# The eight steps of a second modulation, moved between the stages of four token blocks

## The chip, the cores and the metric

The kernel runs on one core of a Trainium2 chip. The metric is the device time of one execution in microseconds (us). "Before" is the kernel as it stood, "after" the one with the change.

## The reference

One layer of a streaming encoder for 2048 prompt tokens and 64 sample tokens, width 1024, all in float32. A vector `c` for each of the two sequences gives six modulation vectors of 1024 values; everything else is per token:

```
mod = silu(c) @ w_ada + b_ada                  # 1024 -> 6 x 1024
sh1, sc1, gt1, sh2, sc2, gt2 = split(mod, 6)
h = rms_norm(x) * (1 + sc1) + sh1
glu_a, glu_b, q, k, v, g_conv, g_attn = split(h @ w_in)
conv = silu(layer_norm(depthwise31(glu_a * sigmoid(glu_b)))) @ w_conv_out
attn = band_attention(norm(q), norm(k), v) @ w_attn_out
x = x + gt1 * ((sigmoid(g_conv) * conv + sigmoid(g_attn) * attn) @ w_o)
h2 = rms_norm(x) * (1 + sc2) + sh2
x = x + gt2 * ((silu(gate) * up) @ w_ffn_out)  # gate, up = split(h2 @ w_ffn_in)
```

`sh1` and `sc1` are needed at once. `gt1`, `sh2`, `sc2` and `gt2`, here called the second modulation, are needed only when all of `q` to `g_attn` has been computed for every token.

## The kernel before

**Stages.** The first half of the program runs over four blocks of tokens (576, then three of 512). A block passes eight stages, given by `ORDER` (line 564): the products q, k and v; four gated products, numbered 0 to 3 (`glu`: two products of 24 matmuls on 512 tokens each, then a tanh gate, after which VectorE adds up the 31 taps of the convolution); and "g", the sixteen gates. They stand in the order q, 0, k, 1, v, 2, 3, g. The second half (merge, output product, feed-forward) comes after all four blocks. A float32 product is made of three matmuls on split operands: a high part `hh`/`whi` in float32r and a low part `hl`/`wlo`.

**Order.** TensorE's instructions stand in the order in which the Python code emits them. While the code emits a product, it keeps an estimate of each engine's load, and at fixed distances it lets other work in (`Stream`, `Lane`): the attention heads of the block before (`sc` scores, `ptp` transposed probabilities, `po` outputs), the norm of the next block (`pt<-ident,x_t`), and the rows of q and k, whose normed form `kn` is transposed back (`pt<-ident,kn`) and stored. So an instruction added or removed on TensorE shifts the places of the rest. The other engines run their own queues in order. Nearly all DMAs are issued from one queue, SyncE's (SP).

**The second modulation.** `mod_steps` is a generator with eight steps, one for each half of the four vectors. A step multiplies four slabs of `w_ada` (`wmod`, 512 KB each, 256 rows by 512 columns) by the two `c` vectors: 16 instructions on TensorE, 32 matmul records in the trace. VectorE copies the sums (`R<-pa`), two small products with `sel` follow some 2.5 us later by the estimate, and VectorE writes one of `B2`, `A2`, `gates_c`. The slabs live in four buffers: `Slabs.free` fills a buffer as soon as the step that used it is done, so the 2 MB for a step are requested right behind the step before it, from SP's queue. The first step's slabs are there long before.

**Where the steps stand.** `MODS` (line 562) says after which stages a step is emitted; the loop over `ORDER` ends with

```
        for _ in range(MODS.get((b, stage), 0)):
            next(mods)
    next(mods)
```

The last `next(mods)` stands behind all stages: it transposes and stores the gates.

**Two buffers for split rows.** `parts()` hands out pairs `part_h`, `part_l` from two buffers (`NS = 2`). ScalarE writes the high part, VectorE the low part, and a pair is free again when its DMA to DRAM has landed. The convolution's last step (`c_d<-part_h`, four of them at the end of a block), the rows of q and k (`q_d`, `k_d`) and the finished heads (`o_d`) all go through these two.

Of the kernel before, what the change touches and what calls it, by code (L numbers as in the profile page):

```python
# [558 lines left out]


MOD_HALVES = [(c6, half) for c6 in (3, 4, 2, 5) for half in range(2)]
MODS = {(b, ct): 1 for b in (1, 2) for ct in range(4)}

ORDER = [(b, st) for b in range(4) for st in ("q", 0, "k", 1, "v", 2, 3, "g")]

# [57 lines left out]
def streaming_layer(ctx: ExitStack, tc: tile.TileContext, I, O):  # L623
# [1024 lines left out]
    for b, stage in ORDER:  # L1648
# [44 lines left out]
        else:  # L1693
# [7 lines left out]
            if stage == 3:  # L1701
# [3 lines left out]
                else:  # L1705
                    tail.add(conv_norm(y, 0, QB, lo))
        for _ in range(MODS.get((b, stage), 0)):
            next(mods)
# [673 lines left out]
```

## Time and profile before

| | before |
|---|---|
| median of 3 runs | 2945.97 us |
| lowest and highest run | 2940.69 and 2946.77 us |
| profiled execution, its own time | 2941.67 us |
| its span, first to last instruction | 2939.5 us |
| TensorE, VectorE, ScalarE, GpSimd busy | 98%, 70%, 46%, 40% of the span |
| TensorE busy between 300 and 960 us | 650.53 of 660 us |
| granted TensorE clock, mean | 0.997 |

Times in the profile count from the start of the span. In a timeline, a row has the start and the duration in us, the engine, the line, the operation, what it writes and reads, and in brackets the idle time of the engine just before it with what ended that. Line 105 is that of a helper that records every instruction, so rows are told apart by the names of their tiles. PE is TensorE, PEld its weight loads, DVE VectorE, ACT ScalarE, POOL GpSimd, SPq SyncE's DMA queue.

### The profile page before, as it was taken

How to read it: one execution, taken by the hardware profiler on the slowest of the kernel's cores; microseconds unless marked ns; L12 is line 12 of the kernel's file. 1: busy time of each engine (PE TensorE's matmuls, PEld its weight loads, DVE VectorE, ACT ScalarE, POOL GpSimd, SP SyncE). 2: the span in 40 equal slices, each digit the busy share in tenths (PEclk: the TensorE clock that was granted, in tenths of full speed). 3: DMA queues.
4: the chain of work that ended last, by engine and by line, in shares of the span. 5: the costliest groups of instructions: out<-in, count | busy, mean ns of one | idle time of the engine just before them, and what ended most of it. 6: DMA issues, size and time to landing. Idle time of an engine off the chain costs nothing.

```text
span 2939.5 us, 44832 instructions
## 1 busy us (share of the span) xinstructions
PE 2889.3 (98%) x16193; PEld 2587.5 (88%) x16193; DVE 2053.9 (70%) x3648; ACT 1362.7 (46%) x2453; POOL 1164.9 (40%) x753
## 2 busy tenths in 40 slices
PE   7999999999999999999999999999999999999999
PEld 5899777888888887988999998999999999999998
DVE  5897788668967885577777756666666557566666
ACT  3346543751564266563444345444444345444442
POOL 1201210111011002553566452366567742465667
PEclk9999999999999999999999999999999999999999
DMA  9989899978996987984444875332333965333333
GB/s 322 315 305 314 287 281 329 285 232 306 285 297 197 320 270 224 291 295 157 144 144 146 292 261 200 97 122 94 115 115 104 346 220 179 97 103 106 115 107 127
DMA packets 467067, 628.04 MB, mean 214 GB/s; under 512 B 36196, under 2 KB 314584, under 8 KB 466845
## 3 DMA queue, kind: packets, MB, share of 16 engines
q1 hardware_dynamic: 452944, 606.11, 63.4%
q10 hardware_dynamic: 13901, 19.08, 1.9%
q8 instruction: 127, 2.08, 0.3%
q14 instruction: 95, 0.78, 0.1%
HBM read 476.53 MB, written 148.54 MB: 213 GB/s over the span
## 4 chain that ended last, share of the span: by engine, by line
PE 47%; DVE 2%; ACT 1%; DMA 1%; issue 1%; POOL 0%; SPq 0%; ACTq 0%; DVEq 0%; POOLq 0%
PE ps L105 29%; PE pd L105 13%; PE pw L105 5%; DVE wlo L105 1%; ACT whi L105 1%; DVE ps L105 0%; DMA cin<-o_d 0%; DMA x<-x_d 0%; DVE acc L105 0%; ACT xn L105 0%; DMA wst<-in_w_ffn_in 0%; DMA wfo<-in_w_ffn_out 0%; DMA tg<-g_d 0%; DVE sums L105 0%; PE pt L105 0%
## 5 line engine op out<-in xcount | busy, mean ns | idle before, releaser
L105 PE MATMUL ps<-t,whi 128*128 128x384 f32 (+1 forms) x2112 | 502.0, 322 | 2.8 <-ACT u L105 1.7
L105 POOL TENSOR_TENSOR wlo<-wst,whi 128x1024 fp32r<-128x1024 f32 (+1 forms) x159 | 362.7, 2293 | 246.1 <-ACT whi L105 214.4
L105 ACT ACTIVATE whi<-wst 128x1024 fp32r<-128x1024 f32 (+1 forms) x265 | 258.3, 979 | 316.1 <-PE ps L105 129.6
L105 PE MATMUL ps<-b,whi 128*128 128x384 f32 (+1 forms) x1584 | 380.7, 325 | 6.4 <-DVE v L105 2.1
L105 PEld LDWEIGHTS ps<-t,whi 128*128 128x128 f32 x2112 | 367.8, 188 | 10.1 <-ACT u L105 3.9
L105 DVE SCALAR_TENSOR_TENSOR y<-u,wd,y 128x512 f32<-128x512 f32 (+1 forms) x480 | 370.1, 774 | 8.0
L105 PE MATMUL ps<-hh,whi 128*128 128x512 f32 (+2 forms) x992 | 362.8, 366 | 0.1
L105 DVE TENSOR_TENSOR acc<-acc,pd 128x512 f32<-128x512 f32 x482 | 322.2, 685 | 48.1 <-PE pd L105 45.6
L105 PE MATMUL ps<-hh,wlo 128*128 128x512 f32 (+2 forms) x992 | 345.2, 348 | 0.0
L105 PE MATMUL ps<-hl,whi 128*128 128x512 f32 (+2 forms) x992 | 344.5, 347 | 0.0
L105 PE MATMUL ps<-t,wlo 128*128 128x384 f32 (+1 forms) x1056 | 338.5, 321 | 0.0
L105 PE MATMUL pd<-whi,hid 128*128 128x512 f32 x912 | 297.9, 391 | 0.6 <-DVE hid L105 0.3
L105 PEld LDWEIGHTS ps<-b,whi 128*128 128x128 f32 x1584 | 276.9, 188 | 14.6 <-DVE v L105 3.2
L105 ACT ACTIVATE pr<-pr,sm 128x640 f32<-128x640 f32 (+3 forms) x272 | 201.9, 749 | 137.1 <-DVE sm L105 134.8
L105 PE MATMUL ps<-b,wlo 128*128 128x384 f32 (+1 forms) x792 | 256.1, 323 | 0.0
L105 POOL TENSOR_TENSOR r<-t,mhalf 128x1 f32<-128x1 f32 (+2 forms) x68 | 82.3, 1219 | 403.7 <-DVE t L105 377.8
L105 PEld LDWEIGHTS ps<-hh,wlo 128*128 128x128 f32 x992 | 186.5, 188 | 22.6
L105 DVE TENSOR_TENSOR wlo<-wst,whi 128x1024 fp32r<-128x1024 f32 (+1 forms) x106 | 135.9, 1286 | 100.3 <-ACT whi L105 98.9
L105 PEld LDWEIGHTS pd<-whi,hid 128*128 128x128 f32 x912 | 171.2, 188 | 37.2 <-DVE acc L105 1.8
L105 PEld LDWEIGHTS ps<-hh,whi 128*128 128x128 f32 x992 | 187.0, 189 | 18.2 <-issue 3.3
L105 PEld LDWEIGHTS ps<-hl,whi 128*128 128x128 f32 x992 | 187.4, 189 | 14.3 <-issue 1.7
L105 PEld LDWEIGHTS ps<-t,wlo 128*128 128x128 f32 x1056 | 198.2, 188 | 0.8
(233 smaller groups left out, 6309.6 us busy)
## 6 DMA issues: line engine op xcount, KB each, us to landing
whi<-w_din_h SPq DMA_DIRECT2D x72, 512.0 KB, 6.4
wlo<-w_din_l SPq DMA_DIRECT2D x72, 512.0 KB, 7.3
wst<-sum_d SPq DMA_DIRECT2D x131, 256.0 KB, 3.1
wfo<-in_w_ffn_out SPq DMA_DIRECT2D x64, 512.0 KB, 4.1
wmod<-in_w_ada SPq DMA_DIRECT2D x46, 512.0 KB, 8.8
sum_d<-ws SPq DMA_DIRECT2D x88, 256.0 KB, 2.0
wst<-in_w_ffn_in SPq DMA_DIRECT2D x85, 256.0 KB, 3.2
wst<-in_w_in SPq DMA_DIRECT2D x40, 512.0 KB, 6.0
```

The source lines that it names most:

```text
L105: self.last = f(*args, **kw)
```

## The change

```
-MODS = {(b, ct): 1 for b in (1, 2) for ct in range(4)}
+MODS = {at: 1 for at in ((0, "g"), (1, 0), (1, 1), (1, 2), (1, "g"), (2, 0), (2, 1), (2, 2))}
```

Before, the steps stand behind the gated products 0, 1, 2, 3 of block 1 (steps 1 to 4) and of block 2 (steps 5 to 8). Now step 1 stands behind the gates of block 0, steps 2 to 4 behind products 0 to 2 of block 1, step 5 behind the gates of block 1, and steps 6 to 8 behind products 0 to 2 of block 2. Behind the products numbered 3 stands none. What a step computes is unchanged, and so is the number of instructions on TensorE.

On TensorE, at the passage from the gates of block 0 (`128x288`, one half of its 576 tokens) to q of block 1 (`128x512`), a piece of the difference reads:

```order
 L105 MATMUL ps<-hl,whi 128x288
 L105 MATMUL ps<-hh,wlo 128x288
-L105 MATMUL ps<-whi,hh 128x512
-L105 MATMUL ps<-wlo,hh 128x512
-L105 MATMUL ps<-whi,hl 128x512
-L105 MATMUL ps<-whi,hh 128x512
-L105 MATMUL ps<-wlo,hh 128x512
-L105 MATMUL ps<-whi,hl 128x512
+L105 MATMUL pa<-wmod,cl 32x256 x16
```

Step 1 now comes before the first matmul of q in block 1; the removed rows are found again behind it.

SP's queue around products 2 and 3 of block 1, before. `whi` and `wlo` are the two parts of a stored weight slab, `wmod` the slabs of a step, `o_d` a finished head:

```order
L479 DMA whi<-w_din_0_h 128x1024
L479 DMA wlo<-w_din_0_l 128x1024
L249 DMA wmod<-in_w_ada 128x2x512 x4
L1460 DMA o_d<-part_h 128x64
L1460 DMA o_d<-part_l 128x64
L479 DMA whi<-w_din_1_h 128x1024
L479 DMA wlo<-w_din_1_l 128x1024
L479 DMA whi<-w_din_0_h 128x1024
L479 DMA wlo<-w_din_0_l 128x1024
L249 DMA wmod<-in_w_ada 128x2x512 x4
```

The same place after:

```order
L1460 DMA o_d<-part_h 128x64
L1460 DMA o_d<-part_l 128x64
L479 DMA whi<-w_din_0_h 128x1024
L479 DMA wlo<-w_din_0_l 128x1024
L249 DMA wmod<-in_w_ada 128x2x512 x4
L479 DMA whi<-w_din_1_h 128x1024
L479 DMA wlo<-w_din_1_l 128x1024
L479 DMA whi<-w_din_0_h 128x1024
L479 DMA wlo<-w_din_0_l 128x1024
```

Before, two groups of four slabs are requested here: for step 4, which stands right behind the next product, and for step 5. Now there is one, for step 5, and its user stands behind the gates of the block.

VectorE's queue at product 0 of block 1, before. `u` is the gated product, `y` a tap of the convolution, `part_l<-ln` the low part of the third and fourth stores to `c_d`, `part_l<-pt` a row of q, `kn` the next row of q that TensorE will transpose:

```order
L105 SCALAR_TENSOR_TENSOR u<-tb,ps 128x512
L105 RECIPROCAL sm<-sm 128x1
L105 TENSOR_SCALAR y<-u,wd,cols 128x512
L105 RECIPROCAL sm<-sm 128x1
L105 COPY R<-pa 128x256
L105 TENSOR_TENSOR part_l<-ln,part_h 128x512 x2
L105 SCALAR_TENSOR_TENSOR part_l<-pt,gqk,part_h 128x512
L105 TENSOR_TENSOR kn<-kn,r 128x512
```

The same place after:

```order
L105 SCALAR_TENSOR_TENSOR u<-tb,ps 128x512
L105 TENSOR_SCALAR y<-u,wd,cols 128x512
L105 SCALAR_TENSOR_TENSOR y<-u,wd,y 128x512
L105 TENSOR_TENSOR part_l<-ln,part_h 128x512
L105 COPY R<-pa 128x256
L105 SCALAR_TENSOR_TENSOR y<-u,wd,y 128x512
L105 TENSOR_TENSOR part_l<-ln,part_h 128x512
L105 SCALAR_TENSOR_TENSOR y<-u,wd,y 128x512
L105 SCALAR_TENSOR_TENSOR part_l<-pt,gqk,part_h 128x512
L105 TENSOR_TENSOR kn<-kn,r 128x512
```

Three taps (`y<-u,wd,y`) now stand ahead of `kn` that stood behind it; two small reciprocals are gone from there; and `R`, which waits for the step's sums, stands behind the first `part_l` instead of ahead of both.

## The prediction

> **What bounds the kernel now.** I read the head of the page first, then the waits of TensorE between 300 and 800 us, where all eight steps stand before and after, then the timelines at the waits. The head of the page gives the span and the busy time of each engine:
>
> ```profile
> span 2939.5 us, 44832 instructions
> PE 2889.3 (98%) x16193; PEld 2587.5 (88%) x16193; DVE 2053.9 (70%) x3648; ACT 1362.7 (46%) x2453; POOL 1164.9 (40%) x753
> ```
>
> TensorE (PE) is busy for 98% of the span, and its work is the same before and after. So the change can only move what TensorE waits for and what the clock gate takes. Its waits between 300 and 800 us, as the total, the count and the longest:
>
> ```profile
> PE pt L105 <- DVE kn L105: 4.0, 1, 4.0
> PE pa L105 <- DMA wmod<-in_w_ada: 2.6, 4, 0.7
> PE sc L105 <- DVE sm L105: 1.6, 2, 1.3
> PE ps L105 <- DVE hl L105: 0.6, 1, 0.6
> ...
> PE pt L105 <- DVE x_t L105: 0.2, 1, 0.2
> ```
>
> Two of them belong to steps. The slabs `wmod` are waited for four times, 2.6 us in all, and the timeline shows that all four stand at one step, number 4, behind product 3 of block 1:
>
> ```profile
> 466.28 0.39 PE L105 MATMUL ps<-hh,wlo 128*128 128x512 f32 x1
> 467.23 0.64 PE L105 MATMUL pa<-wmod,cl 128*32 128x256 f32 x8 [0.56 <-DMA wmod<-in_w_ada]
> 468.49 0.64 PE L105 MATMUL pa<-wmod,cl 128*32 128x256 f32 x8 [0.62 <-DMA wmod<-in_w_ada]
> 469.82 0.64 PE L105 MATMUL pa<-wmod,cl 128*32 128x256 f32 x8 [0.69 <-DMA wmod<-in_w_ada]
> 471.19 1.08 PE L105 MATMUL pa<-wmod,cl 128*32 128x256 f32 x8 [0.73 <-DMA wmod<-in_w_ada]
> 472.20 0.80 PE L105 MATMUL ps<-hh,whi 128*128 128x512 f32 x1
> ```
>
> Products and slabs come from one queue (SP). It requests a step's four slabs right behind the step before. These are the requests for steps 3 and 4:
>
> ```profile
> 416.62 2.43 SPq L249 DMA_DIRECT2D wmod<-in_w_ada  x4
> 457.12 3.14 SPq L249 DMA_DIRECT2D wmod<-in_w_ada  x4
> ```
>
> Step 4's request stands at 457.12 to 460.26 and its first matmul is due at 466.51 (the last product matmul at 466.28 and one spacing of 0.23): 9.4 us from the first slab and 6.3 us from the last. What a slab takes there, from the DMA view between 440 and 480 us (KB each, and the median time to landing):
>
> ```profile
> q1 hardware_dynamic: 6546, 14.49, 102.3%
> wmod<-in_w_ada SPq DMA_DIRECT2D x8, 512.0 KB, 10.1
> ```
>
> A slab lands after 10.1 us in a queue that is full, and the step asks after 9.4. The other steps are not waited for.
>
> **The change, part by part.** *Step 4 moves from behind product 3 to behind product 2.* Before, the step took until 472.20. Without a wait a step takes as long as step 1 behind product 0, the first two of these rows, which also show the wait for `kn`:
>
> ```profile
> 353.73 1.94 PE L105 MATMUL pa<-wmod,cl 128*32 128x256 f32 x32
> 355.59 0.50 PE L105 MATMUL ps<-whi,hh 128*128 128x512 f32 x1
> ...
> 356.16 0.39 PE L105 MATMUL ps<-whi,hl 128*128 128x512 f32 x1
> 360.51 0.63 PE L105 MATMUL pt<-ident,kn 128*128 128x128 f32 x4 [3.96 <-DVE kn L105]
> ```
>
> 355.59 - 353.73 = 1.86 us. So step 4 should have ended at 466.51 + 1.86 = 468.37 and ended at 472.20, 3.83 us late. The windows from 466.51 on add the clock (busy times with counts, then PEclk, the share of the DMA engines and GB/s):
>
> ```profile
> 356.39:360.51 4.12, 0.16 (x1) 0.03 (x1) 2.51 (x4) 1.46 (x3) 0.00 (x0) 1.00 0.77 206
> 361.56:368.39 6.83, 6.83 (x24) 5.86 (x23) 4.71 (x11) 3.13 (x6) 0.00 (x0) 0.50 1.08 387
> 466.51:470.80 4.29, 2.07 (x25) 0.50 (x24) 3.17 (x7) 1.75 (x3) 0.67 (x1) 1.00 1.06 397
> 470.80:474.21 3.41, 3.02 (x14) 1.92 (x15) 0.42 (x1) 0.00 (x0) 0.00 (x0) 0.50 1.03 413
> 480.00:490.00 10.00, 10.00 (x52) 8.33 (x51) 10.00 (x19) 5.44 (x10) 0.45 (x1) 1.00 0.78 202
> ```
>
> From 470.80 to 474.21 the clock was 0.50. The part behind 472.20, 2.01 us, did half the work: another 1.0. This whole stall, 4.8 us, is at stake. Afterwards step 4 stands where step 3 stood, and step 3 where step 2 stood. The slabs of step 4 are then requested about as step 3's were, at 416.62, for a use at about 452.54:
>
> ```profile
> 452.54 1.29 PE L105 MATMUL pa<-wmod,cl 128*32 128x256 f32 x20
> ```
>
> That is 36 us against 10.1. What hides them is a whole product and the stage v; if that cover went, they would cost up to the 3.8 again. Every other step has as long: step 5 stands behind the gates, a product later than step 4, whose 144 matmuls of 0.23 us alone are 33 us, and steps 6 to 8 repeat 2 to 4. I take **-4.8**; the bounds are 0 and -4.8.
>
> The Trainium skill (TensorE: Matmul & The Clock Gate, "HAM oscillation — how this bites in real kernels") says that the clock falls when TensorE idles for more than about 3.4 us on end; by it this term is -3.8, since the longest gap here is 0.73 us. The trace disagrees: 0.50 was granted after a stretch in which TensorE was busy for 2.07 of 4.29 us in short pieces. At `kn`, where the gap is 3.96 us, rule and trace agree.
>
> *Step 1 moves to the gates of block 0.* It adds 1.86 us ahead of q of block 1. The slabs have been there from the start. The norm's waits `hl` 0.6 and `x_t` 0.2 stand near this passage, and 1.86 us of TensorE's work ahead of them gives their engines time: **-0.8**, bounds 0 and -0.8.
>
> *Step 2 stands where step 1 stood, and the wait for `kn` behind it is looked at again.* TensorE came at 356.39 (356.16 and a spacing) and waited until 360.51 for VectorE. What VectorE and ScalarE did there:
>
> ```profile
> 354.32 0.68 DVE L105 SCALAR_TENSOR_TENSOR u<-tb,ps 128x512 f32<-128x512 f32 x1
> 356.17 0.69 DVE L105 TENSOR_TENSOR part_l<-ln,part_h 128x512 fp32r<-128x512 f32 x1
> 357.19 0.69 DVE L105 TENSOR_TENSOR part_l<-ln,part_h 128x512 fp32r<-128x512 f32 x1 [0.33 <-ACT part_h L105]
> 359.02 0.75 DVE L105 SCALAR_TENSOR_TENSOR part_l<-pt,gqk,part_h 128x512 fp32r<-128x512 f32 x1 [1.13 <-ACT part_h L105]
> 359.68 0.68 DVE L105 TENSOR_TENSOR kn<-kn,r 128x512 f32<-128x512 f32 x1
> 358.26 0.69 ACT L105 ACTIVATE part_h<-pt,gqk 128x512 fp32r<-128x512 f32 x1 [1.10 <-DMA c_d<-part_h]
> 362.54 0.69 ACT L105 ACTIVATE part_h<-pt,gqk 128x512 fp32r<-128x512 f32 x1 [3.59 <-DMA c_d<-part_h]
> ```
>
> `kn` stands behind a `part_l` that needs a `part_h`, which waits for one of the two buffers, that is for a store to `c_d` to land. The stores were issued at these times:
>
> ```profile
> 356.16 0.32 SPq L1350 DMA_DIRECT2D c_d<-part_h  x1
> ...
> 357.80 0.41 SPq L1350 DMA_DIRECT2D c_d<-part_h  x1
> ```
>
> The first freed its buffer after 2.1 us (358.26 - 356.16), the second after 4.7 (362.54 - 357.80). After the change three more taps stand ahead of `kn`, at the mean of their group (busy total, mean ns, idle ahead):
>
> ```profile
> L105 DVE SCALAR_TENSOR_TENSOR y<-u,wd,y 128x512 f32<-128x512 f32 (+1 forms) x480 | 370.1, 774 | 8.0
> ```
>
> 3 x 0.77 = 2.3 us more. They fill VectorE's idle 0.33 + 1.13 = 1.5 us; `u`, which started 0.59 us behind the product's end at 353.73, no longer has a score and a reciprocal ahead of it in a row, for 0.5 or so. That leaves about **+0.3**: TensorE still waits, for 4.3 us, and the clock still falls (0.50 over 6.83 us, at most 3.4 lost). The bounds are far apart. If the queue has caught up before `u`, the 4.1 of wait and 3.4 of clock go, -7.5. If the stores land late, it costs more: pairs of parts from 300 to 400 us took
>
> ```profile
> DMA to landing us min/median/max: 4.6/7.1/8.1
> ```
>
> from issue to landing. That is the slower rival below. I stay at +0.3, because the rows at this very place give it.
>
> *The catch-up behind product 3.* While TensorE stalled at step 4, VectorE got 3.83 us in which it fell no further behind. In 480 to 490 it is busy for 10.00 of 10.00 us. Without the stall the scores and heads of the next stage could find it late: between 0 and +3.8. The nearest row for what such a wait costs is `sc <- sm`, 1.6 us over two; the two waits stand over 500 us of similarly full stretches, so I take **+0.3**.
>
> The sum: -4.8 - 0.8 + 0.3 + 0.3 = -5.0. The profiled execution took 2941.67 us by its own time (2939.5 of span and 2.2 around it), 4.3 below the median of the three runs, 2945.97, which spread from 2940.69 to 2946.77. I take the sum from the middle of the two, 2943.8: **2938.8 us**.
>
> The Trainium skill (DMA: Bandwidth & Descriptors, "Anatomy of one DMA — SWDGE (gpsimd) path") puts a transfer at 2.0 us and its bytes at 436 GB/s, 3.2 us for a slab of 512 KB. By it the last slab of step 4, requested by 460.26, would have landed by 463.5, ahead of 466.51, and the term would be nil. The queue is another one, and the trace disagrees: 10.1 us, and four waits.
>
> **The rivals.** *B: the wait for `kn` goes too.* For it: the third and fourth stores may go out earlier. Against it: three more taps. Price at best -7.5 - 0.3 more than the forecast, 2931.0; half of it, with the wait below what makes the clock fall, 2935.
>
> *C: the step's stall is given back.* VectorE's lack of reserve in 480 to 490 turns most of the 4.8 into waits for `sm` and `pl` behind product 3. For it: 10.00 of 10.00. Against it: of 200 us with such stretches only 1.9 us of waits came from it. The net is -1 to 0, about 2943.
>
> *D: slower, by the two buffers.* In the new order a request for a 512 KB slab of the products stands among the halves of the stores to `c_d`. If the two stores then land after 7.1 to 8.1 us instead of 2.1 and 4.7, the chain to `kn` is later by (8.1 - 2.1) + (8.1 - 4.7) = 9.4 us. Then the stall falls into two, one for each store, and a second stretch at clock 0.50 like that of 6.83 us loses 3.4 more: +12.8 at this place. With the 5.3 saved elsewhere (4.8 + 0.8 - 0.3 for the catch-up) the net is +7.5, 2951.3; half as much again at step 6 in block 2, whose place is alike, makes 2957. Slower than the median by over 0.2% it is from 13.1 above the forecast, which needs a little of the second place. For it: the queue is at 0.77 to 1.08 in these very rows. Against it: the second late store delayed nothing of TensorE's before, since `kn` for it had passed.
>
> *E: the change does not do what it says.* The wait for slabs goes from step 4 to another step: 2943.
>
> **How the numbers follow.** About 0.2%, 5.9 us, is what a measurement of this kernel can tell from no change (its runs differ by 6.1). The bounds are 2940.1 and 2951.9 against the median. The forecast, 0.50, lies 1.3 us below the lower one: 0.33 faster, 0.17 same. B 0.15 is faster. C 0.09 and E 0.02 are same. D 0.24 is slower: with the second place it clears the bound by far, and without it it reaches 2951.3, where a queue a little later decides. Together 0.48 faster, 0.28 same, 0.24 slower. The range goes from B's best, 2931.0, to D at its first place alone, 2951.5; D's upper part, 0.17, and little of the rest lie outside.
>
> **What would show it.** Right: TensorE's waits between 300 and 800 us hold no `wmod`; the clock stays at 1.00 behind product 3 of block 1; the wait for `kn` behind product 0 is still there at 4 to 4.5 us; `hl` and `x_t` are gone. Wrong, faster: no wait for `kn` (B). Wrong, slower: a wait for `kn` of over 8 us, or one in block 2, released by `part_h` after a store to `c_d` (D); or new waits for `sm` and `pl` at 470 to 500 (C).

## The result: slower, and the profile after

| | before | after |
|---|---|---|
| median of 6 runs each, beside one another | 2944.61 us | 2954.56 us |
| lowest and highest | 2940.69 and 2946.77 | 2950.42 and 2955.94 |
| ratio, 95% interval | | 1.0036 (1.0024 to 1.0047) |
| profiled execution, its span | 2939.5 | 2948.5 |

The changed kernel is about 10 us slower. The head of its page shows that no engine has more to do:

```profile
span 2948.5 us, 44833 instructions
PE 2889.5 (98%) x16193; PEld 2586.4 (88%) x16193; DVE 2053.3 (70%) x3648; ACT 1363.8 (46%) x2453; POOL 1165.5 (40%) x753
```

TensorE is busy for 2889.5 us, as before for 2889.3. Nearly all of the 9 us between the two spans are waits. TensorE's waits between 300 and 800 us after the change:

```profile
PE sc L105 <- DMA kk<-k_d: 5.9, 1, 5.9
PE sc L105 <- DVE sm L105: 4.8, 3, 3.2
PE pt L105 <- DVE kn L105: 3.6, 1, 3.6
PE sc L105 <- issue: 0.9, 1, 0.9
...
PE ps L105 <- DMA wlo<-w_dqkv_l: 0.2, 1, 0.2
```

The waits for `wmod`, `hl` and `x_t` that stood here are gone, as meant. In their place stand a wait of 5.9 us for `kk`, the load of a head's keys, and one of 3.2 us for `sm`, a score bank that VectorE has not freed yet. The timeline gives the places: `sm` in q of block 1, the known wait for `kn` behind product 0, and `kk` in the gates of block 1:

```profile
345.27 0.51 PE L105 MATMUL sc<-kk,q 128*128 128x256 f32 x2 [3.17 <-DVE sm L105]
368.92 0.63 PE L105 MATMUL pt<-ident,kn 128*128 128x128 f32 x4 [3.65 <-DVE kn L105]
492.05 1.41 PE L105 MATMUL sc<-kk,q 128*128 128x320 f32 x4 [5.87 <-DMA kk<-k_d]
```

The clock fell behind each of the three, as the windows show (the last three columns are PEclk, DMA share, GB/s):

```profile
345.80:349.21 3.41, 3.41 (x10) 2.75 (x10) 0.94 (x5) 1.44 (x4) 0.00 (x0) 0.50 0.97 326
369.69:373.10 3.41, 3.41 (x12) 2.75 (x11) 1.61 (x3) 1.67 (x3) 0.00 (x0) 0.50 1.08 306
489.15:495.98 6.83, 3.93 (x12) 3.37 (x13) 1.58 (x5) 0.69 (x1) 1.41 (x2) 0.50 0.84 254
```

Half of the busy time in them was lost: 1.7, 1.7 and 2.0 us. The loss behind `kn` was there before, with 3.4 us; the other two are new.

To compare kernels closer than their total times allow, I use the passage in which they differ. TensorE's matmul records have the same order in all of them up to number 1950 of 16193 (in the gates of block 0) and in the last 10698 (from the gates of block 2 on). The table has the time from the start of record 1950 to that of the first of the last 10698, and in it TensorE's idle time and half of its busy time in stretches at clock 0.50, worked out from the traces.

| profile | passage us | idle | lost to the clock |
|---|---|---|---|
| before, first and second | 654.5, 653.4 | 9.1, 9.4 | 4.9, 3.4 |
| after, first and second | 662.8, 668.0 | 16.8, 18.7 | 5.4, 8.9 |

In the first profiles 8.3 of the 9.0 us lie in this passage: 7.7 of idle time and 0.5 of clock. The second pair (n1_before and n2_after, below) has the same long waits at the same places (after the change `sm` 3.5, `kn` 3.6 and `kk` 5.9 us), so they belong to the order and not to one execution; what varies is mostly the clock.

### The profile page after: what moved, and what is told of

Its sections match the earlier page's. It is cut to its first block, busy times and chain, and to the rows that moved or that the text cites. A ratio compares the mean times of both kernels' runs of the same rounds, so it can differ in the third digit from the quotient of the medians.

```text
span 2948.5 us, 44833 instructions
## 1 busy us (share of the span) xinstructions
PE 2889.5 (98%) x16193; PEld 2586.4 (88%) x16193; DVE 2053.3 (70%) x3648; ACT 1363.8 (46%) x2453; POOL 1165.5 (40%) x753
## 4 chain that ended last, share of the span: by engine, by line
PE 47%; DVE 2%; DMA 1%; ACT 1%; issue 1%; POOL 0%; SPq 0%; ACTq 0%; DVEq 0%
PE ps L105 29%; PE pd L105 13%; PE pw L105 5%; DVE wlo L105 1%; ACT whi L105 0%; DVE ps L105 0%; DMA x<-x_d 0%; DMA cin<-o_d 0%; DMA wst<-in_w_conv_out 0%; ACT xn L105 0%; DVE acc L105 0%; DMA wfo<-in_w_ffn_out 0%; DMA tg<-g_d 0%; DVE sums L105 0%; PE pt L105 0%
## 5 line engine op out<-in xcount | busy, mean ns | idle before, releaser
L105 POOL TENSOR_TENSOR r<-t,mhalf 128x8 f32<-128x8 f32 (+2 forms) x68 | 83.8, 1240 | 404.0 <-DVE t L105 379.8
```

What stands on the lines that cost most here:

```text
L105: self.last = f(*args, **kw)
```

## The experiments

**Parts of the change.** Each moves only some of the steps; all else is as before. Step 1 and the steps of block 2 get the places that the change gives them. Step 4 does not: the change puts it behind product 2, which step 3 leaves, while here it goes behind the gates. What the two have in common is that no step stands behind product 3 of block 1. No part moves steps 2 and 3.

```
step 4:   MODS at (1,0) (1,1) (1,2) (1,"g")      (2,0) (2,1) (2,2) (2,3)
step 1:   MODS at (0,"g") (1,1) (1,2) (1,3)      (2,0) (2,1) (2,2) (2,3)
block 2:  MODS at (1,0) (1,1) (1,2) (1,3) (1,"g") (2,0) (2,1) (2,2)
step 5:   MODS at (1,0) (1,1) (1,2) (1,3) (1,"g") (2,1) (2,2) (2,3)
```

Step 4 alone: 

> Only step 4 moves, from behind product 3 of block 1 to behind its gates; steps 1 to 3 and 5 to 8 stand as before, so TensorE's order is that of before up to 466 us. Theory (each move has its own price, and this is the one that gains): the four waits for wmod and the clock loss behind them go, 3.8 + 1.0 = -4.8 us against before, about 2939.8; no wait for kk in the gates, since no slabs of a step are requested there ahead of the loads of q and kk. Rival (any shift of the order of the attention heads behind product 3 makes a new wait): the wmod waits go but waits for sm or kk of 3 to 8 us appear between 470 and 540 us, 2943 to 2948.

Step 1 alone: 

> Only step 1 moves, from behind product 0 of block 1 to behind the gates of block 0; steps 2 to 8 stand as before. Theory (the move of step 1 makes the wait for sm in q of block 1): a wait of sc for sm of about 3.2 us near 345 us with half clock behind it (1.7 us), step 4's waits for wmod still there; 3 to 5 us above before, 2947.5 to 2949.5. Rival (the wait for sm in the changed kernel comes from the place of step 2, behind product 0, or from chance): no wait above 1 us for sm near 345, and 0.8 us below before, 2943.8.

The steps of block 2: 

> Only the steps of block 2 move: step 5 to behind the gates of block 1, steps 6 to 8 to behind products 0 to 2 of block 2; steps 1 to 4 stand as before, with the waits for wmod at step 4. Theory: nothing in block 2 waits before or after; the small waits that the changed kernel has behind 600 us (0.9, 1.3 and 0.6) come with this part, so 0 to 2.4 us above before, 2944.6 to 2947. Rival (the wait for kk in the gates of block 1 belongs to step 5's new place): a wait for kk of 4 to 6 us near 490, 2951 or more.

Of these, step 5 alone: 

> Only step 5 moves, from behind product 0 of block 2 to behind the gates of block 1; steps 1 to 4 and 6 to 8 stand as before. With all four steps of block 2 moved the time was 5 us above before. Theory (step 5 is the one that costs, by 1.86 us ahead of the norm and q of block 2, as step 1 does in block 1): 3 to 5 us above before, with waits for x_t, hl or sm between 590 and 680 us. Rival (steps 6 to 8, each a product earlier, cost it): no change, within 1.5 us of before.

| moved | ratio to before (95%) | passage | idle | clock |
|---|---|---|---|---|
| step 4 | 0.9992 (0.9983 to 1.0001) | 652.9 | 10.0 | 1.7 |
| step 4, repeated | 0.9990 (0.9981 to 0.9999) | 655.7 | 10.2 | 5.8 |
| step 1 | 1.0024 (1.0012 to 1.0035) | 660.9 | 14.8 | 4.4 |
| steps of block 2 | 1.0017 (1.0008 to 1.0026) | 655.8 | 11.0 | 3.4 |
| step 5 | 1.0006 (0.9997 to 1.0015) | 659.2 | 12.3 | 6.4 |

With 2944 us as 1, step 4 is worth -2.4 and, repeated (

> Step 4 alone moved, once more. If its gain is real, 2 to 4 us below before again; if the first comparison was chance, within 1.5 us of before.

), -2.9 us; step 1 costs +7.1; the steps of block 2 cost +5.0. With the mean of the first two that is +9.5 together, against +10.6 by the ratio for the whole change. That does not show the change to be the sum of its parts. Besides the place of step 4, its longest wait, 5.9 us for `kk`, stands in none of them: near 490 us only step 1's part has one, of 1.3 us. What is shown is the sign of each: an empty place behind product 3 gains a little, and the two other moves lose.

Step 1 brings the wait for `sm` and a longer one for `kn`, as the first four rows of its waits between 300 and 800 us show:

```profile
PE sc L105 <- DVE sm L105: 6.3, 6, 3.4
PE pt L105 <- DVE kn L105: 5.5, 1, 5.5
PE pa L105 <- DMA wmod<-in_w_ada: 1.4, 2, 0.7
PE sc L105 <- DMA kk<-k_d: 1.3, 1, 1.3
```

The 5.5 is the 4.0 of before and the 1.86 us of the step that no longer stands ahead of it, less 0.4. In the change itself step 2 stands there, and the wait for `kn` is 3.6; so not all of the 7.1, which is above the expected 3 to 5, belongs to the change. In step 4's rows, here the first three of the repeat, there is no `wmod`, but 3.2 us for `kk` have come:

```profile
PE pt L105 <- DVE kn L105: 4.0, 1, 4.0
PE sc L105 <- DMA kk<-k_d: 3.2, 2, 2.0
PE sc L105 <- DVE sm L105: 2.2, 2, 1.3
```

The move takes the wait away, not the full queue behind it. Where the gain of 2.4 to 2.9 us lies, the profiles do not show: their idle time, 10.0 and 10.2 us, is no less than before. The two executions that were profiled took 2945.32 and 2942.89 us, each the longest of its eleven.

For the steps of block 2, 0 to 2.4 us above before were expected, or a wait for `kk` near 490; the time was 5.0 us above, and no profile has that wait. The profiled execution took 2942.09 us, the least of its eleven, so two more were made: 

> The four steps of block 2 moved, a second profile. Theory (the part has small waits of its own in block 2, for x_t, sm and kk, that vary with the phase in which transfers land): 3 to 6 us of waits and half clock more than before between 470 and 965 us. Rival (its loss lies outside, at the start or behind 965 us): that passage within 1.5 us of before.

 

> The four steps of block 2 moved, a third profile, with the same expectations as for the second.

 Their passages took 656.8 and 660.9 us (idle 11.9 and 13.1; clock 4.1 and 6.7). Before, TensorE waited for nothing that the view lists between 590 and 965 us; in the slower of the two:

```profile
PE pt L105 <- DVE x_t L105: 2.1, 1, 2.1
PE sc L105 <- DMA kk<-k_d: 1.1, 1, 1.1
PE sc L105 <- DVE sm L105: 1.0, 1, 1.0
```

These three stand in the other profiles of this part as well, between 0.4 and 1.2 us each. The chance of a half-clock stretch comes on top. Step 5 alone has only the one for `kk` of the three, 1.9 us, so by its one profile the others come with steps 6 to 8. It has no wait for `x_t`, `hl` or `sm` there, which its theory expected, and its time, 1.8 us above before by the ratio, lies between the two expectations. The longest of the three passages (660.9) fits the theory, the shortest (655.8) the rival, the third lies between; some of the 5 us is not placed.

**The wait for kk.** Two edits of the changed kernel. The first delays the request for step 5's slabs:

```
-        self.stream.at(self.stream.when("pe"), ...
+        self.stream.at(self.stream.when("pe") + (15000 if 28 < self.given <= 32 else 0), ...
```

> The changed kernel, but the slabs of step 5 are requested 15 us later by the planner's estimate, so that the loads of q and kk in the gates of block 1 come with no step's slabs right ahead of them. Both theories of the wait for kk (the queue's eight places, of which the gate's store held one; or the 2 MB of slabs that keep the DMA engines full) expect the wait of 5.9 us near 490 and the half clock behind it (2.0 us) to go: 7.9 us below the changed kernel, about 2946.7. Rival (kk is late because it is asked for earlier in the new order): the wait stays above 3 us, 2950 or more.

The second issues one DMA, the first gate's store of block 1, from SP behind the loads of q, kk and vv:

```
+            if (b, g) == (1, 0):
+                with tc.issue_after(now["kk"].ins):
+                    nc.sync.dma_start(g_d[...], t[...])
```

> The changed kernel, but one DMA, the first gate's store of block 1, is issued from SP behind the loads of q and kk and of vv instead of from ScalarE ahead of them. The bytes are the same; only what stands eight DMAs ahead of the second kk is now the last wmod slab instead of that store. Theory (at most eight DMAs are out, and each request waits for the one eight places ahead; the store held kk back from 479.7 to 488.3): kk is requested at about 480, the wait of 5.9 us near 492 falls to about 3, as its neighbours take 8 to 10 us to land in the full queue; 2.9 to 5 us below the changed kernel, about 2950 to 2951.5. Rival (the bytes of the slabs alone make kk late): the wait stays at 5 to 6 us, 2954.

Why that store: SP's waits after the change, between 476 and 490 us, and the four requests of that head:

```profile
SPq L1430 <- DMA g_d<-gate: 8.6, 1, 8.6
SPq L1429 <- DMA wmod<-in_w_ada: 1.8, 2, 1.0
SPq L1430 <- DMA wmod<-in_w_ada: 0.7, 1, 0.7
```

```profile
476.47 0.61 SPq L1429 DMA_DIRECT2D q<-q_d  x1
477.78 0.47 SPq L1430 DMA_DIRECT2D kk<-k_d  x1
479.12 0.60 SPq L1429 DMA_DIRECT2D q<-q_d  x1
488.33 0.45 SPq L1430 DMA_DIRECT2D kk<-k_d  x1
```

After the second `q`, SP could have gone on at 479.7. A load of keys has no data in common with a store of gates. But in the program all DMAs of SP and ScalarE take turns at eight completion semaphores (in the trace numbers 100 and 102 to 108, 232 or 233 DMAs each), so each waits until the one eight places ahead has landed; here that was the store, at 488.3.

With the slabs later, the wait for `kk` in the gates went; TensorE's only wait between 470 and 500 us was

```profile
PE sc L105 <- DVE sm L105: 1.0, 1, 1.0
```

The time did not follow, against the 7.9 us expected: ratio 1.0036 (1.0023 to 1.0048), passage 662.9. A wait for `kk` of 2.2 us came at 511 and one for `x_t` of 1.4 at 870, and the stretches at half clock behind the waits for `sm` and `kn` cost 7.2 us instead of the 5.4 of all stretches after the change. This edit does not tell the two theories apart; both expected this wait to go. With the store moved, the request went out early and the wait hardly changed:

```profile
482.02 0.60 SPq L1433 DMA_DIRECT2D q<-q_d  x1
483.37 0.45 SPq L1434 DMA_DIRECT2D kk<-k_d  x1
494.91 1.40 PE L105 MATMUL sc<-kk,q 128*128 128x320 f32 x4 [4.70 <-DMA kk<-k_d]
```

After the change TensorE asked at 492.05 - 5.87 = 486.18, 2.15 us ahead of the request; here at 494.91 - 4.70 = 490.21, 6.84 us behind it. The request is 9.0 us earlier against TensorE, the wait 1.2 us shorter: the load now takes up to 11.5 us (483.37 to 494.91) instead of 3.7. So my theory of the eight places holds for the request and is wrong in size for the wait, and in this run the rival, the bytes, has most of it: four slabs and four weights, 4 MB, are requested within 9 us ahead of these loads. Before, eight requests of the same kinds went out from 463.39 to 472.70, but the first load of the head followed at 479.76; after the change it follows the last of them by 1 us, at 476.47. The ratio, 1.0043 (1.003 to 1.0056), is no better than the changed kernel's.

The landings after the change, between 466 and 492 us, say the same without an edit:

```profile
q<-q_d SPq DMA_DIRECT2D x2, 256.0 KB, 9.7
kk<-k_d SPq DMA_DIRECT2D x2, 256.0 KB, 10.3
```

The second `q` was requested at 479.12 and landed 9.7 us later, at 488.8; the first `kk` landed at 488.1. Both were late for TensorE, which asked at 486.18. So by an estimate from these landings at least 2.6 of the 5.9 us would have been waited without the hold.

The same from the other side, with four tiny loads in the kernel before, three of which come between the store and `kk` and put it eight places behind:

```
+        if (x, h) == (1, 1):
+            for i in range(4):
+                nc.sync.dma_start(tiny[:, 4 * i : 4 * i + 4], I["c_sample"][0:1, 4 * i : 4 * i + 4])
```

> The kernel before, with four loads of 16 bytes each added on SP at the gates of block 1: one ahead of the first gate's store, three between it and the loads of q and kk, so that the second kk stands eight places behind the store, as in the changed kernel. TensorE's order is that of before. Theory (eight places): the second kk, at 481.71 before, is requested only when the store has landed, at about 488, lands 3.5 us later, and TensorE, which asks at 489.8, waits about 2 us for it; 2 to 4 us above before, 2945.5 to 2947.5. Rival (the store's place does not matter): kk is requested at 482 to 484, no wait, 2943.5.

Of SP's four requests for that head, the last three became

```profile
481.47 0.54 SPq L1435 DMA_DIRECT2D kk<-k_d  x1
485.29 0.60 SPq L1434 DMA_DIRECT2D q<-q_d  x1
487.24 0.45 SPq L1435 DMA_DIRECT2D kk<-k_d  x1
```

The second `kk` goes out at 487.24, 5.5 us later than before, behind a wait for `g_d`; but TensorE asked at 491.1 and did not wait, since the load needed less than the 3.9 us. The ratio was 1.0010 (1.0002 to 1.0019), while the profile, of an execution of 2943.88 us, the least of its eleven, shows no new wait (passage 654.7); where those 3 us are is not shown.

**The wait for sm.** Two edits of the changed kernel, again. In the first, GpSimd does 32 of 512 columns of four products and leaves the rest out:

```
-            gps.tensor_tensor(yv[:, ct], yv[:, ct], s[:, :n], ALU.mult)
+            if t0 == SMP:
+                stream.add("pool", "tensor_tensor", n, (ALU.mult,), {})
+                nc.gpsimd.tensor_tensor(yv[:, ct, :32], yv[:, ct, :32], s[:, :32], ALU.mult)
```

> The changed kernel with one part of the work left out: the four products y by s of the convolution's norm of block 0 on GpSimd cover 32 of 512 columns, 0.3 us instead of 1.3 to 1.4 each. The order on the other engines is that of the changed kernel. Theory (the wait for sm in q of block 1 is the end of a chain in VectorE's queue, to which GpSimd adds: kn took 1.76 us instead of 0.68 while GpSimd ran, and it started behind an r that stood behind three of these products): the wait of 3.17 us near 345 falls to about 2, and the half clock behind it (1.7 us) may go; 1 to 3 us below the changed kernel, 2951.5 to 2953.5. Rival (GpSimd has no part in it): the wait stays above 3 us, 2954.

`kn` on VectorE, first after the change, then here, and TensorE's wait here:

```profile
340.53 1.76 DVE L105 TENSOR_TENSOR kn<-kn,r 128x512 f32<-128x512 f32 x1
```

```profile
341.77 0.68 DVE L105 TENSOR_TENSOR kn<-kn,r 128x512 f32<-128x512 f32 x1
345.64 0.51 PE L105 MATMUL sc<-kk,q 128*128 128x256 f32 x2 [2.07 <-DVE sm L105]
```

The wait fell by 1.1 us, as much as `kn` became shorter, and the half clock behind it went. The ratio, 1.0030 (1.0019 to 1.0041), is 1.8 us below the changed kernel's, within both intervals. These products are a third of the wait; the rest ends by the profile with VectorE, and what makes it there was not tested by this edit.

In the second, step 1 stands one stage later, at (1,"q") instead of (0,"g"): 

> The changed kernel, but step 1 stands one stage later, behind q of block 1 instead of behind the gates of block 0. Theory (the wait for sm comes from step 1 standing ahead of q, where it shifts block 0's scores against the convolution's norm): no wait for sm above 1 us near 345, hl and x_t wait 0.6 and 0.2 as before; 3.2 + 1.7 - 0.8 = 4 us less than the changed kernel. In this order the gate's store stands eight places ahead of vv, not of kk, so the wait for kk should be 2 us or less: another 4 to 6 us, 2944 to 2946 in all. Rival (it is the number of steps ahead of product 0 of block 1 that counts, not their place): a wait for sm or kn of 3 us more than before remains, 2948 to 2951.

The wait for `sm` was gone, no `kk` was waited for up to 500 us, and the ratio was 1.0006 (0.9997 to 1.0015). Of all edits of the changed kernel this is the one that won back most of the loss. But another wait had grown, as TensorE's, VectorE's and SP's rows show:

```profile
366.31 1.09 PE L105 MATMUL pt<-ident,kn 128*128 128x128 f32 x4 [8.12 <-DVE kn L105]
364.82 0.75 DVE L105 SCALAR_TENSOR_TENSOR part_l<-pt,gqk,part_h 128x512 fp32r<-128x512 f32 x1 [3.52 <-DMA c_d<-part_l]
346.00 3.16 SPq L249 DMA_DIRECT2D wmod<-in_w_ada  x4
```

Step 2's slabs are now requested at 346, right ahead of the stores to `c_d` from 349 on, and VectorE stands idle for 3.5 us until one of these stores has landed. This is the mechanism of the prediction's slower rival, with a step's slabs in place of the products', in another order than the one it was made for.

**A version with two gains in view.** Step 4 alone moved, and `kn` of the q rows no longer pinned behind the row before:

```
-        with tc.issue_after(dve.last.ins):
+        with tc.issue_after(dve.last.ins) if col < PBLOCKS[0][1] or dst is k_d else nullcontext():
```

> Step 4 alone moved, as in the first experiment, and in addition the products kn of the q rows from block 1 on are no longer held behind the row before on VectorE, so that they stand ahead of the stores to c_d and their two buffers. TensorE's order is that of the first experiment. Theory (kn is late because it stands behind a part that waits for a buffer): the wait for kn of 4.0 us at 360 and the half clock behind it go, 5 to 7 us below the first experiment, 2934 to 2936. Rival (the convolution's norm, pushed back behind kn, makes a new wait in its place): 2939 to 2941, no gain over the first experiment.

```profile
PE sc L105 <- DVE sm L105: 7.0, 4, 3.8
PE pt L105 <- DVE x_t L105: 1.0, 2, 0.8
PE ps L105 <- DVE part_l L105: 0.7, 1, 0.7
```

The wait for `kn` of 4.0 us went, and waits for `sm` of 7.0 us, 2.2 with step 4 alone, took its place: ratio 1.0019 (1.0010 to 1.0028). The rival was nearer, and still too hopeful. Step 4 alone, 2940.59 and 2939.79 us against 2943.36 and 2943.34 of before, is the one version whose times lie below both kernels', by 1 in 1000. The first comparison's interval still touches no change, the second's just misses it, and no profile shows the gain.

The two profiles for the spread of the passage: 

> The kernel before once more, for a second profile: how far the passage from the gates of block 0 to the end of block 2's gates, where the orders of TensorE differ, varies from one execution to the next. In the first profile it took 654.5 us. Expected: the same waits, within 2 us, the difference being stretches at half clock of 3.4 us that come or stay away with the phase of the gate.

 

> The changed kernel once more, for a second profile. In the first the same passage took 662.8 us. Expected if the waits that the first profile shows are the order's own: again sm 3.2, kn 3.6 and kk 5 to 6 us, and 661 to 665 us. If they were chance of that execution: other places, and within 3 us of before.

 Both came out so, but for the second of after, whose 668.0 is above the range: it has 3.5 us more lost to the clock, and waits for `x_t` (1.6) and `ptp` (1.3) that the first does not show.

## Why the prediction was wrong

Two terms failed most. The catch-up term (+0.3) asked only VectorE what a faster step 4 would meet and put SP's queue at nothing: there the wait for `kk` cost 5.9 us and 2.0 of clock. Step 1's term (-0.8) counted the two waits that go and put at nothing what comes behind the step: 3.2 us for `sm` and 1.7 of clock. Block 2, put at nothing as well, cost 2.4 in this profile. The places in the passage, from the first profile of each kernel, as idle time and loss to the clock in us:

| place | before | after | forecast | measured |
|---|---|---|---|---|
| step 4, `wmod` | 2.6 and 1.5 | none | -4.8 | -4.1 |
| `hl` and `x_t` ahead of q of block 1 | 0.8 | none | -0.8 | -0.8 |
| `sm` in q of block 1 | none | 3.2 and 1.7 | none | +4.9 |
| `kn` behind product 0 | 4.0 and 3.4 | 3.6 and 1.7 | +0.3 | -2.1 |
| `kk` in the gates of block 1 | none | 5.9 and 2.0 | none | +7.9 |
| `sm` and `pl` behind product 3 | none | none | +0.3 | 0.0 |
| waits behind 600 us (`sm`, `wlo`, "issue") | none | 2.4 | none | +2.4 |
| other waits for `sm` | 1.6 | 1.6 | none | 0.0 |

These add up to +8.2, against 8.3 of the passage.

**Step 4, -4.8.** The mechanism was right: no `wmod` is waited for after the change. The slabs are requested from 423.27 on and used at 458.69, 35 us later, against 36 forecast. The stall itself went, in the table 4.1 of the 4.8, since that counts idle time and clock alone. One part of it was less sure than it looked: the second profile of before has the same four waits and no half clock behind them. (The 144 matmuls that the prediction gives a product are 48 in the trace; nothing hangs on it, as step 5's slabs have 151 us.) In the part with step 4 behind the gates, the time fell by 2.4 to 2.9 us.

**Step 1, -0.8.** The two small waits did go, and I stopped there. I did not ask what 1.86 us of TensorE's work ahead of q does to the places of the scores and the convolution's norm in the other queues. A score now comes 3.2 us too early for VectorE, and 1.7 us of clock go with it; the step alone, with nothing in its old place, cost 7.1. That the step's place makes this wait is shown both ways: it came with step 1 alone and went with the step behind q. My own sentence, that the planner sets all of this by estimated loads, applied to this place as it did to `kn`.

**`kn`, +0.3.** Right in the mechanism: still there, 3.65 and 3.61 us, against 4.3 forecast and 3.96 before, with half clock behind it. VectorE has no idle time left between `u` at 362.55 and `kn` at 368.09, so the taps filled it as forecast. That the clock took 1.7 and 2.6 us in the two profiles and not 3.4 differs from one execution to the next: with step 4 alone moved, the same wait cost 1.7 once. The rival without the wait (B) did not come.

**Catch-up, +0.3.** Wrong resource. After the change no `sm` or `pl` is waited for between 470 and 500 us: rival C did not come. The wait there is for a load. The row that warned was quoted, 102.3% of the DMA engines between 440 and 480 us, and I used it only for the slabs. Who takes a wait away in a stretch where the queue is full has to ask which load is asked for next.

**Block 2, nothing.** I moved steps 5 to 8 at no cost, because nothing waited there before. Moved alone they cost +5.0. A stretch with no waits is not one with room: small waits came up as soon as the order moved.

**D, slower.** The forecast's slower case had the right sign, with a cause that did not act in this kernel: no store to `c_d` held `kn` back. It acted in the variant with step 1 behind q, at 8.1 us. The range ended at 2951.5, where D's first place alone would lie. The result, 2954.56, needed three losses (step 1, `kk`, block 2) that I had priced at nothing or at a gain.

## What to carry to other kernels

In a kernel whose TensorE is busy for 98% of the time, the waits that a profile shows are not the only places without room; VectorE's queue and the DMA queue stood close behind in the edits tried here, and nearly every wait taken away brought up another. So price a moved piece of work at its old place, at its new one, and in the first urgent load and the first score behind each. And move one piece at a time: here the one part that gained, 1 in 1000, was a single step, and the longest wait of the whole change stood in none of the parts that were run alone.

## What the runs showed of the hardware

GpSimd can slow VectorE: `kn` took 1.76 us beside one of GpSimd's wide products (`y<-y,s`) and 0.68 without. It does not do so always: in the same trace `kn` took 0.69 beside GpSimd's `r`, and `hl` 0.67 while such a product ran.

The clock can fall after several short waits as after a long one, and whether it does differs between executions of one kernel: behind the four waits for `wmod` it fell in the first profile of before and not in the second. The passage lost 4.9 and 3.4 us to it before, 5.4 and 8.9 after. Behind a wait of 3 to 4 us the loss was 1.7 us (`kn` in the first profile of step 4's part) to 4.3 us (`sm` in the version with both edits), so it can be as large as the wait.

A DMA can wait for one that it has nothing to do with: SP was free to request `kk` at 479.7 and did so at 488.33, behind a store of gates eight places ahead. In a full queue the earlier request bought 1.2 us for 9.0.
